# Channels outermost, heads innermost in the column blocks of a projection

## The chip, the cores and the metric

The kernel runs on one core of a Trainium2 chip. The metric is the device time of one execution in microseconds; of several runs the median counts.

## What is computed

One block of a diffusion backbone with 2048 latent tokens (`x`), a prefix of 256 context tokens (`ctx`) and 1024 channels: eight heads of a bidirectional RWKV-7 scan beside a gated short convolution, then a mixture of 16 experts that choose their tokens. The change touches only the first step, the projection, and what it leaves in DRAM for the scan. In short:

```python
px = modulate(rmsnorm(x, norm1_g), sh1, sc1) @ w_in        # the same for ctx
xr, xk, xv, xw, xa, xgl = split_rwkv(px_rw, mu, grid_shift(px_rw, rows))   # 512, 512, 512, 64, 64, 128 columns
kk = k * k_k;  kk = kk / max(sqrt(sum(kk * kk over a head)), 1e-12)
for d in (forward, backward):
    wl = -softplus(-(w0[d] + tanh(xw) @ w_up[d])) - 0.5
    a = sigmoid(a0[d] + xa @ a_up[d])
    kd = k * (1 + (a - 1) * k_a)
    y, s = wkv_scan(s0, r, exp(-exp(wl)), kd, v, -kk, kk * a, reverse=d)
bonus = sum(r * k_sum * r_k over a head) * v
...
x = x + g1 * (concat(a_x, b_x) @ w_out);  x = x + g2 * expert_choice_ffn(...);  return rmsnorm(x, final_g)
```

`grid_shift` moves channel 4i+t of a column to the left, right, upper or lower neighbour token, by its t.

## The kernel before

**Layout.** The projection keeps channels on the 128 partitions and tokens along the free dimension. On the host, `layout` reorders the columns of `w_in` into blocks of 128 (lines 1599 to 1608): block 0 holds the low-rank columns xw and xa, blocks 1 to 4 the keys, 5 to 8 the receptances, 9 the gate, 10 to 13 the values. The order inside a block is the list `tm` (line 1599): the shift t is outermost, so that a block has one shift direction, then the head h, then i, so that channel 4i+t of head h stands on partition 16h + i. The constants `mu`, `kk`, `ka`, `rk`, `w0`, `a0` follow the same list, and so do the columns of the low-rank matrices `wup2` and `aup2` (lines 1622 and 1623), whose rows are put in the order `perm64`.

**The passes.** `proj_phase` runs four passes of 512 tokens (the context's 256 go with the first). Each pass normalises and splits its tokens into a high and a low part (`prep_tile`), then runs 14 blocks: `load_block` (line 241) fetches the block's weights in two halves of 256 KB (tile `wr`, two buffers, line 247), ScalarE rounds them to `wH` (line 129), VectorE takes the rest as `wL` (line 134), and `block_mm` multiplies (line 262). What follows a block is queued and comes one block later: `post_wa`, `post_k`, `post_r` with `post_kd`, `post_g`, `post_v`. A timeline scheduler fixes the order of each engine's instructions when the program is built.

**The row stores.** `post_r` and `post_kd` leave in DRAM what the scan reads: `NR` (line 487; tiles `nrb` and `nrs`), and for both directions `C` (line 516; tile `ct`, two buffers) and `KBD` (line 517; tile `bk`, two buffers). A row there is one channel of one head over all 2304 tokens: 2304 floats in `C`, 2 x 2304 in `NR` and `KBD`. The destination's pattern is made by `to_heads` (line 373): the tile has 128 partitions, the DRAM side eight heads (64 rows apart) by 16 channels by the tokens. A buffer of `bk` is written first by VectorE at line 512, and may be written again once its store has landed; for `ct` that is the scan at line 508. All these DMAs are issued by the sync engine (SP), in program order, on one hardware queue that has the weight loads too, the stores `HS` of the normalised tokens (line 368), and the loads of `x`. In a pass the stores of blocks 5 to 8 follow one another, one block behind their blocks.

**The low-rank loads.** `post_wa` stores block 0 to `WA` (line 439) and reads it back twice onto two halves of 64 partitions (line 444), once for xw and once for xa; there the DRAM side has four shifts by 16 rows by the tokens.

**The values.** `post_v` turns values from channels on partitions to tokens on partitions (line 549), into a PSUM tile whose free order is shift, head, i. ScalarE copies it to the order head, shift, i (line 551), and it is stored to `V`.

Two small matrices pick heads: `bones` (128 x 128, ones where two partitions have the same head; line 322) and `hsel` (128 x 8; line 320), both from the partition number shifted right by four.

Of the kernel before, what the change touches and what calls it, by code (L numbers as in the profile page):

```python
# [7 lines left out]
F32 = mybir.dt.float32  # L8
# [5 lines left out]
OP = mybir.AluOpType  # L14
# [5 lines left out]
NTOK = T + TC  # L20
# [4 lines left out]
H = 8  # L25
# [17 lines left out]
def _dap(t, off, ap):  # L43
    a = t[tuple(slice(None) for _ in t.shape)] if not isinstance(t, bass.AP) else t
    return bass.AP(tensor=a.tensor, offset=a.offset + off, ap=ap)
# [220 lines left out]
def proj_phase(ctx_, tc, k, I, S, fill):  # L266
    nc = tc.nc
    bp = k.bp
    with ExitStack() as ctx:
# [42 lines left out]
        pi = pool.tile([128, 1], I32, name="pi", bufs=1)  # L312
# [1 line left out]
        bones = pool.tile([128, 128], F32, name="bones", bufs=1)  # L314
        hsel = pool.tile([128, H], F32, name="hsel", bufs=1)
        nc.gpsimd.iota(pi, pattern=[[1, 1]], base=0, channel_multiplier=1)
        nc.vector.tensor_scalar(pi, pi, 4, None, op0=OP.logical_shift_right)
        nc.vector.tensor_copy(pf, pi)
        nc.gpsimd.iota(jp, pattern=[[1, 128]], base=0, channel_multiplier=0)
        nc.vector.tensor_scalar(hsel, jp[:, 0:H], pf, None, op0=OP.is_equal)  # L320
        nc.vector.tensor_scalar(jp, jp, 4, None, op0=OP.logical_shift_right)
        nc.vector.tensor_scalar(bones, jp, pf, None, op0=OP.is_equal)
        up = pool.tile([128, 2, 2, 512], F32R, name="up", bufs=1)
        gupH = pool.tile([128, 512], F32R, name="gupH", bufs=1)
# [48 lines left out]
        def to_heads(t, j, mult, t0, n):  # L373

            w = mult * NTOK
            return _dap(t, j * 16 * w + mult * t0, [[64 * w, H], [w, 16], [1, mult * n]])

        def evac_lat(b, p, ps):
            e = pool.tile([128, 11, PR], F32, name="e")
# [51 lines left out]
        def post_wa(units, es):  # L431

            n0 = units[0][0]
            xx = [[pool.tile([128, 704], F32R, name="x" + nm + part, bufs=1) for part in "HL"] for nm in "wa"]
            for u, e in zip(units, es):
                t0, n, _ = u
                q = pool.tile([128, 512], F32, name="q")
                mixed(0, u, e, r64(q[:, :n]))
                nc.sync.dma_start(S["WA"][:, t0:t0 + n], q[:, :n])
                cs = slice(t0 - n0, t0 - n0 + n)  # L440
                for z in range(2):
                    q = pool.tile([128, 512], F32, name="q")
                    for half in range(2):
                        nc.sync.dma_start(q[64 * half:64 * half + 64, :n],
                                          _dap(S["WA"], 16 * z * NTOK + t0, [[32 * NTOK, 4], [NTOK, 16], [1, n]]))
                    if z == 0:
                        nc.scalar.activation(q[:, :n], q[:, :n], AF.Tanh)
                    split(k, nc, xx[z][0][:, cs], xx[z][1][:, cs], q[:, :n], "dve")
            xwa["x"], xwa["o"] = xx, n0
# [85 lines left out]
        def post_v(j, units, es):  # L535
            for u, e in zip(units, es):
                t0, n, _ = u
                big = n > 256
                if j == 0:
                    st["v", t0] = pool.tile([128, 4, 512 if big else 256], F32, name="kq" + "sb"[big], bufs=1)  # L540
                vq = st["v", t0]
                mixed(10 + j, u, e, r64(vq[:, j, :n]))
                if j < 3:
                    continue
                for a in range(0, n, 128):
                    m = min(128, n - a)
                    ps = psum.tile([128, 4, H, 16], F32, name="pw")
                    for i in range(4):
                        nc.tensor.transpose(ps[:m, i].rearrange("p h c -> p (h c)"), vq[:, i, a:a + m], k.ident)
                    v = pool.tile([128, H, 4, 16], F32, name="vt", tag="sg", bufs=2)  # L550
                    nc.scalar.copy(v[:m].rearrange("p h g c -> p g h c"), ps[:m])
                    vf = v.rearrange("p h g c -> p (h g c)")
                    nc.sync.dma_start(S["V"][t0 + a:t0 + a + m, :], vf[:m])
                    if t0 < TC:
                        continue
                    w = pool.tile([128, 512], F32, name="vb", tag="a", bufs=2)
                    nc.gpsimd.tensor_tensor(w[:m].rearrange("p (h c) -> p h c", c=C), v[:m].rearrange("p h g c -> p h (g c)"),
                                            st["o", t0][:m, a // 128].unsqueeze(2).to_broadcast([m, H, C]), op=OP.mult)
                    nc.vector.tensor_tensor(w[:m], w[:m], gn[:m, 1], op=OP.add)
                    nc.vector.tensor_tensor(w[:m], w[:m], st["g", t0][:m, a // 128], op=OP.mult)  # L560
                    nc.sync.dma_start(S["VB"][t0 - TC + a:t0 - TC + a + m, :], w[:m])
# [1019 lines left out]
def layout(inputs):  # L1581
    import numpy as np
    f = lambda n: np.asarray(inputs[n], dtype=inputs[n].dtype)
    g = {}
    perm64 = np.concatenate([np.arange(i, 64, 4) for i in range(4)])
    pm = lambda n: np.concatenate([perm64 + 64 * i for i in range(n // 64)])
    p512 = pm(512)
    g["x"] = np.ascontiguousarray(f("x").reshape(T, D))
    g["ctx"] = np.ascontiguousarray(f("ctx").reshape(TC, D))
    col = lambda v: np.asarray(v).reshape(-1, 128).T  # L1590
    ada_w, ada_b = f("ada_w")[0], f("ada_b")[0]
    g["ada_a"] = np.ascontiguousarray(ada_w[:, :2048].reshape(KT, 128, 2048))
    parts = [3, 4, 2, 5]
    g["ada_b"] = np.ascontiguousarray(
        np.stack([ada_w[:, o * 1024 + q * 512:o * 1024 + q * 512 + 512].reshape(KT, 128, 512) for o in parts
                  for q in range(2)]))
    g["ada_rows"] = np.ascontiguousarray(np.stack([ada_b[2048:3072], ada_b[5120:6144]]))
    w = f("w_in")[0]
    tm = np.array([h * 64 + 4 * i + t for t in range(4) for h in range(8) for i in range(16)])
    rw = np.concatenate([np.array([1536 + 64 * z + 4 * i + t for t in range(4) for z in range(2) for i in range(16)]),  # L1600
                         512 + tm, tm, np.array([1664 + 4 * i + t for t in range(4) for i in range(32)]), 1024 + tm])
    wr = w[:, :1792][:, rw]
    blocks = [wr[:, 128 * b:128 * b + 128] for b in range(14)]
    for j in range(4):
        for o in (2, 1, 0):
            s = 1792 + 512 * o + 128 * j
            blocks.append(w[:, s:s + 128])
    g["w_in"] = np.ascontiguousarray(np.stack([b.reshape(KT, 128, 128).transpose(1, 0, 2) for b in blocks]))
    mub = f("shift_mu")[0][rw]
    c = np.stack([f("c")[0].reshape(KT, 128), f("c_ctx").reshape(KT, 128)], axis=-1).transpose(1, 0, 2).reshape(128, 16)  # L1610
    cols = {"c": c, "adab_a": col(ada_b[:2048]), "adab_b": col(ada_b[3072:5120]), "n1": col(f("norm1_g")[0]),
            "n2": col(f("norm2_g")[0]), "mu": col(mub), "kk": col(f("k_k")[0][tm]), "ka": col(f("k_a")[0][tm]),
            "rk": col(f("r_k")[0].reshape(512)[tm]),
            "w0": np.concatenate([col(f("w0")[0, d][tm]) for d in range(2)], axis=1),
            "a0": np.concatenate([col(f("a0")[0, d][tm]) for d in range(2)], axis=1),
            "cw": np.concatenate([col(f("conv_w")[0, q]) for q in range(3)], axis=1)}
    colv = np.zeros((128, NCOLV), np.float32)
    for n, (a, b) in COLV.items():
        colv[:, a:b] = cols[n]
    g["colv"] = colv  # L1620
    dup = lambda u: np.ascontiguousarray(np.concatenate([u, u], axis=0))
    g["wup2"] = dup(f("w_lora_up")[0][:, perm64][:, :, tm].transpose(1, 0, 2))
    g["aup2"] = dup(f("a_lora_up")[0][:, perm64][:, :, tm].transpose(1, 0, 2))
    g["gup"] = np.ascontiguousarray(f("g_lora_up")[0][[4 * i + t for t in range(4) for i in range(32)]][:, p512])
    g["gnrows"] = np.ascontiguousarray(np.stack([f("gn_g")[0][p512], f("gn_b")[0][p512]]))
    g["router"] = np.ascontiguousarray(f("router_w")[0].reshape(KT, 128, NE).transpose(1, 0, 2))
    wo = f("w_out")[0]
    g["w_out"] = np.ascontiguousarray(np.concatenate([wo[:512][p512], wo[512:]]).reshape(KT, 128, D))
    for n, m in (("w_gate", "exp_w_gate"), ("w_up", "exp_w_up")):
        w = f(m)[0].reshape(NE, KT, 128, FB, 128).transpose(0, 3, 2, 1, 4)  # L1630
        g[n] = np.ascontiguousarray(w.reshape(NE, FB, 128, 1024))
    g["w_down"] = np.ascontiguousarray(f("exp_w_down")[0].reshape(NE, FB, 128, D))
    g["final_g"] = np.ascontiguousarray(f("final_g").reshape(1, D))
    return g
# [23 lines left out]
```

## Time and profile before

| | us |
|---|---|
| median of three runs | 3195.19 |
| lowest and highest of them | 3183.33, 3208.47 |
| the profiled execution | 3213.07 |
| its span from first to last instruction | 3211.1 |

The profiled execution is one execution of its own; the mean granted clock of TensorE in it is 0.921 of full speed. Its page lists for each engine the busy time, and the share of the 16 DMA engines' time in which they moved something. The projection takes the first 680 us of the span, the scan with its fillers goes to about 1930, the experts take the rest. PE is TensorE, DVE VectorE, ACT ScalarE, POOL GpSimd, SPq the sync engine's queue of issues.

### The profile page before, as it was taken

The numbers are of one execution on the slowest core, as the hardware profiler recorded it, in microseconds if no ns is written. First come the engines' busy times: TensorE is split into PE (matmuls) and PEld (weight loads), VectorE is DVE, ScalarE is ACT, GpSimd is POOL, SyncE is SP. The second block draws the span as 40 slices with busy tenths as digits, with TensorE's granted clock in tenths as the row PEclk, the third lists the DMA queues.
The fourth block names the chain that finished last, engine by engine and source line by source line (L and its number), as shares of the span: only waits on it lengthen the run. The fifth ranks groups of instructions, "written<-read, shape, count | busy, mean of one in ns | idle before, by whom it ended". The sixth has DMA issues, their size and how long they took to land. (4 is left out here: it accounts for less than half of the span.)

```text
span 3211.1 us, 62585 instructions
## 1 busy us (share of the span) xinstructions
PE 2904.7 (90%) x24367; PEld 2629.1 (82%) x24367; DVE 2136.1 (67%) x4611; ACT 1385.1 (43%) x2279; POOL 662.0 (21%) x893
## 2 busy tenths in 40 slices
PE   6878889878999998999999994999999999999997
PEld 4867778768888888877888873989999898999886
DVE  7567766758766666657767746666666666666766
ACT  6446554433344443323454433444444444444443
POOL 0132332443133323212222121001000000001001
PEclk8989899978799999998888986999999999999998
DMA  6355544575556665766566553566666666666786
GB/s 242 122 161 169 196 159 144 177 220 135 137 157 174 158 177 134 222 178 181 140 157 158 122 140 85 168 200 207 220 191 198 192 201 192 208 204 209 262 269 223
DMA packets 407497, 577.43 MB, mean 180 GB/s; under 512 B 174616, under 2 KB 256664, under 8 KB 406176
## 3 DMA queue, kind: packets, MB, share of 16 engines
q1 hardware_dynamic: 396256, 533.58, 54.9%
q0 software_dynamic: 10656, 38.80, 5.3%
q8 instruction: 191, 3.13, 0.4%
q14 instruction: 106, 0.87, 0.1%
q10 hardware_dynamic: 288, 1.05, 0.1%
HBM read 444.73 MB, written 128.59 MB: 179 GB/s over the span
## 5 line engine op out<-in xcount | busy, mean ns | idle before, releaser
L129 ACT CAST wH<-wr 128x1024 fp32r<-128x1024 f32 (+1 forms) x592 | 529.1, 897 | 907.3 <-PE pg L1429 409.4
L134 DVE TENSOR_TENSOR wL<-wr,wH 128x1024 fp32r<-128x1024 f32 (+1 forms) x586 | 625.7, 1072 | 363.4 <-ACT wH L129 358.4
L1429 PE MATMUL pg<-xH,wH 128*128 128x256 f32 x2048 | 587.8, 287 | 18.3 <-ACT s L1433 18.3
L1429 PE MATMUL pg<-xL,wH 128*128 128x256 f32 x2048 | 578.5, 283 | 0.0
L1429 PE MATMUL pg<-xH,wL 128*128 128x256 f32 x2048 | 578.1, 282 | 0.0
L262 PE MATMUL pj<-hH,wH 128*128 128x256 f32 x1600 | 482.1, 302 | 42.8 <-ACT wH L129 22.1
L262 PE MATMUL pj<-hH,wL 128*128 128x256 f32 x1600 | 472.5, 296 | 21.3 <-DVE wL L134 21.2
L262 PE MATMUL pj<-hL,wH 128*128 128x256 f32 x1600 | 471.6, 295 | 1.4 <-DVE hL L134 1.1
L1429 PEld LDWEIGHTS pg<-xH,wH 128*128 128x128 f32 x2048 | 392.1, 192 | 20.4 <-ACT s L1433 19.0
L1429 PEld LDWEIGHTS pg<-xL,wH 128*128 128x128 f32 x2048 | 391.5, 191 | 1.5
L1429 PEld LDWEIGHTS pg<-xH,wL 128*128 128x128 f32 x2048 | 391.9, 191 | 0.0
L262 PEld LDWEIGHTS pj<-hH,wH 128*128 128x128 f32 x1600 | 322.2, 201 | 56.7 <-ACT wH L129 26.3
L262 PEld LDWEIGHTS pj<-hH,wL 128*128 128x128 f32 x1600 | 320.0, 200 | 29.1 <-DVE wL L134 27.0
L262 PEld LDWEIGHTS pj<-hL,wH 128*128 128x128 f32 x1600 | 321.7, 201 | 5.7 <-DVE hL L134 2.0
L1488 POOL DMA_INDIRECT ACC<-o,it x30 | 52.0, 1732 | 968.9 <-DVE o L1474 809.4
L1446 PE MATMUL pd<-wH,hL 128*128 128x512 f32 x512 | 201.9, 394 | 0.0
L1446 PE MATMUL pd<-wL,hH 128*128 128x512 f32 x512 | 201.9, 394 | 0.0
L1446 PE MATMUL pd<-wH,hH 128*128 128x512 f32 x512 | 199.9, 394 | 0.0
L818 DVE TENSOR_TENSOR x<-X,x 128x120 f32<-128x120 f32 (+12 forms) x540 | 157.0, 294 | 58.3 <-DMA X<-TI 46.6
L820 DVE TENSOR_TENSOR X<-X,x 128x120 f32<-128x120 f32 (+12 forms) x540 | 164.8, 308 | 12.3
L782 PE MATMUL pg<-ar,bk 64*128 64x128 f32 x1152 | 136.3, 316 | 21.8 <-DVE g L784 8.1
L782 PEld LDWEIGHTS pg<-ar,bk 64*128 64x128 f32 x1152 | 110.1, 209 | 38.2 <-issue 13.9
(428 smaller groups left out, 5467.1 us busy)
## 6 DMA issues: line engine op xcount, KB each, us to landing
wr<-in_w_gate_dram SPq DMA_DIRECT2D x128, 512.0 KB
wr<-in_w_up_dram SPq DMA_DIRECT2D x128, 512.0 KB
wr<-in_w_down_dram SPq DMA_DIRECT2D x128, 512.0 KB
wr<-in_w_in_dram SPq DMA_DIRECT2D x208, 256.0 KB
bk<-KBD SPq DMA_DIRECT2D x36, 512.0 KB
ar<-NR SPq DMA_DIRECT2D x36, 512.0 KB
adaw<-in_ada_b_dram SPq DMA_DIRECT2D x32, 512.0 KB
inc<-C SPq DMA_DIRECT2D x36, 256.0 KB
```

The source lines that it names most:

```text
L129: nc.scalar.copy(H_, src)
L134: (leng or nc.vector).tensor_tensor(L_, src, H_.bitcast(F32), op=OP.subtract)
L262: nc.tensor.matmul(ps, wa[:, kw, :], ha[:, kt, :], start=m == 0, stop=m == 3 * KT - 1)
L782: nc.tensor.matmul(pg[:, p], bk[rows, p], ar[rows, p], start=True, stop=True)
L818: nc.vector.tensor_tensor(tv, X[:, 0:r, t:t + 1].to_broadcast([128, r, m]), x[:, t:t + 1, t + 1:].to_broadcast([128, r, m]), op=OP.mult)
L820: nc.vector.tensor_tensor(X[:, 0:r, t + 1:], X[:, 0:r, t + 1:], tv, op=OP.add)
L1429: nc.tensor.matmul(ps, a[:, ws], b[:, kt], start=i == 0, stop=i == 23)
L1446: nc.tensor.matmul(po[2 * m + n], a[:, f, ms], b[:, ns], start=f == 0 and q == 0, stop=f == FB - 1 and q == 2)
L1488: nc.gpsimd.indirect_dma_start(out=S["ACC"], out_offset=bass.IndirectOffsetOnAxis(ap=ids[m][:, :1], axis=0), in_=o, in_offset=None, comput ...
```

## The change

The list `tm` now has i outside and h inside: channel 4i+t of head h stands on partition 8i + h. All else follows from that. `to_heads` writes 16 channels by eight heads by the tokens; every row goes to the place in DRAM where it went before. The low-rank load reads 16 rows by four shifts by the tokens, so that the 64 partitions have the channels in their natural order, and `wup2` and `aup2` lose the row order `perm64`. The head of a partition is its number modulo 8 (`bitwise_and` with 7 in place of the shift). The PSUM tile of the transposed values has the free order shift, i, head, and the copy out of it reads in steps of eight elements.

```diff
--- before.py
+++ after.py
@@ -314,11 +314,11 @@
         bones = pool.tile([128, 128], F32, name="bones", bufs=1)
         hsel = pool.tile([128, H], F32, name="hsel", bufs=1)
         nc.gpsimd.iota(pi, pattern=[[1, 1]], base=0, channel_multiplier=1)
-        nc.vector.tensor_scalar(pi, pi, 4, None, op0=OP.logical_shift_right)
+        nc.vector.tensor_scalar(pi, pi, H - 1, None, op0=OP.bitwise_and)
         nc.vector.tensor_copy(pf, pi)
         nc.gpsimd.iota(jp, pattern=[[1, 128]], base=0, channel_multiplier=0)
         nc.vector.tensor_scalar(hsel, jp[:, 0:H], pf, None, op0=OP.is_equal)
-        nc.vector.tensor_scalar(jp, jp, 4, None, op0=OP.logical_shift_right)
+        nc.vector.tensor_scalar(jp, jp, H - 1, None, op0=OP.bitwise_and)
         nc.vector.tensor_scalar(bones, jp, pf, None, op0=OP.is_equal)
         up = pool.tile([128, 2, 2, 512], F32R, name="up", bufs=1)
         gupH = pool.tile([128, 512], F32R, name="gupH", bufs=1)
@@ -373,7 +373,7 @@
         def to_heads(t, j, mult, t0, n):
 
             w = mult * NTOK
-            return _dap(t, j * 16 * w + mult * t0, [[64 * w, H], [w, 16], [1, mult * n]])
+            return _dap(t, j * 16 * w + mult * t0, [[w, 16], [64 * w, H], [1, mult * n]])
 
         def evac_lat(b, p, ps):
             e = pool.tile([128, 11, PR], F32, name="e")
@@ -442,7 +442,7 @@
                     q = pool.tile([128, 512], F32, name="q")
                     for half in range(2):
                         nc.sync.dma_start(q[64 * half:64 * half + 64, :n],
-                                          _dap(S["WA"], 16 * z * NTOK + t0, [[32 * NTOK, 4], [NTOK, 16], [1, n]]))
+                                          _dap(S["WA"], 16 * z * NTOK + t0, [[NTOK, 16], [32 * NTOK, 4], [1, n]]))
                     if z == 0:
                         nc.scalar.activation(q[:, :n], q[:, :n], AF.Tanh)
                     split(k, nc, xx[z][0][:, cs], xx[z][1][:, cs], q[:, :n], "dve")
@@ -544,11 +544,11 @@
                     continue
                 for a in range(0, n, 128):
                     m = min(128, n - a)
-                    ps = psum.tile([128, 4, H, 16], F32, name="pw")
+                    ps = psum.tile([128, 4, 16, H], F32, name="pw")
                     for i in range(4):
-                        nc.tensor.transpose(ps[:m, i].rearrange("p h c -> p (h c)"), vq[:, i, a:a + m], k.ident)
+                        nc.tensor.transpose(ps[:m, i].rearrange("p c h -> p (c h)"), vq[:, i, a:a + m], k.ident)
                     v = pool.tile([128, H, 4, 16], F32, name="vt", tag="sg", bufs=2)
-                    nc.scalar.copy(v[:m].rearrange("p h g c -> p g h c"), ps[:m])
+                    nc.scalar.copy(v[:m].rearrange("p h g c -> p g h c"), ps[:m].rearrange("p g c h -> p g h c"))
                     vf = v.rearrange("p h g c -> p (h g c)")
                     nc.sync.dma_start(S["V"][t0 + a:t0 + a + m, :], vf[:m])
                     if t0 < TC:
@@ -1596,7 +1596,7 @@
                   for q in range(2)]))
     g["ada_rows"] = np.ascontiguousarray(np.stack([ada_b[2048:3072], ada_b[5120:6144]]))
     w = f("w_in")[0]
-    tm = np.array([h * 64 + 4 * i + t for t in range(4) for h in range(8) for i in range(16)])
+    tm = np.array([h * 64 + 4 * i + t for t in range(4) for i in range(16) for h in range(8)])
     rw = np.concatenate([np.array([1536 + 64 * z + 4 * i + t for t in range(4) for z in range(2) for i in range(16)]),
                          512 + tm, tm, np.array([1664 + 4 * i + t for t in range(4) for i in range(32)]), 1024 + tm])
     wr = w[:, :1792][:, rw]
@@ -1619,8 +1619,8 @@
         colv[:, a:b] = cols[n]
     g["colv"] = colv
     dup = lambda u: np.ascontiguousarray(np.concatenate([u, u], axis=0))
-    g["wup2"] = dup(f("w_lora_up")[0][:, perm64][:, :, tm].transpose(1, 0, 2))
-    g["aup2"] = dup(f("a_lora_up")[0][:, perm64][:, :, tm].transpose(1, 0, 2))
+    g["wup2"] = dup(f("w_lora_up")[0][:, :, tm].transpose(1, 0, 2))
+    g["aup2"] = dup(f("a_lora_up")[0][:, :, tm].transpose(1, 0, 2))
     g["gup"] = np.ascontiguousarray(f("g_lora_up")[0][[4 * i + t for t in range(4) for i in range(32)]][:, p512])
     g["gnrows"] = np.ascontiguousarray(np.stack([f("gn_g")[0][p512], f("gn_b")[0][p512]]))
     g["router"] = np.ascontiguousarray(f("router_w")[0].reshape(KT, 128, NE).transpose(1, 0, 2))
```

The instructions and their order stay as they were on PE, DVE, ACT and POOL, and on the sync engine too; what differs there is the pattern of the row stores. The first place is the start of the row stores in the first pass, in the sync engine's order; `nrs` and `nrb` are the context's and the latents' tiles of line 487, `ct` and `bk` those of lines 516 and 517, and the numbers are the outermost count, the next one and the elements of a row. Before:

```order
L444 DMA q<-WA 64x1x448 x4
L247 DMA wr<-in_w_in_dram 128x512 x8
L487 DMA NR<-nrs 8x16x512 x4
L247 DMA wr<-in_w_in_dram 128x512 x2
L516 DMA C_66<-ct 8x16x256
L517 DMA KBD_64<-bk 8x16x512
L247 DMA wr<-in_w_in_dram 128x512
L516 DMA C_67<-ct 8x16x256
L487 DMA NR<-nrb 8x16x896 x2
```

After, at the same place:

```order
L444 DMA q<-WA 64x1x448 x4
L247 DMA wr<-in_w_in_dram 128x512 x8
L487 DMA NR<-nrs 16x8x512 x4
L247 DMA wr<-in_w_in_dram 128x512 x2
L516 DMA C_66<-ct 16x8x256
L517 DMA KBD_64<-bk 16x8x512
L247 DMA wr<-in_w_in_dram 128x512
L516 DMA C_67<-ct 16x8x256
L487 DMA NR<-nrb 16x8x896 x2
```

No row moved: the stores have 16 by 8 rows in place of 8 by 16, and the weight loads stand between the same stores. The low-rank loads are listed by their partitions, so their rows read alike.

The second place is the third pass, 512 tokens, on the sync engine, where weight loads alternate with the stores of the first receptance block. Before:

```order
L516 DMA C_66<-ct 8x16x512
L247 DMA wr<-in_w_in_dram 128x512
L487 DMA NR<-nrb 8x16x1024
L247 DMA wr<-in_w_in_dram 128x512
L516 DMA C_67<-ct 8x16x512
L487 DMA NR<-nrb 8x16x1024
L517 DMA KBD_64<-bk 8x16x1024
```

After:

```order
L516 DMA C_66<-ct 16x8x512
L247 DMA wr<-in_w_in_dram 128x512
L487 DMA NR<-nrb 16x8x1024
L247 DMA wr<-in_w_in_dram 128x512
L516 DMA C_67<-ct 16x8x512
L487 DMA NR<-nrb 16x8x1024
L517 DMA KBD_64<-bk 16x8x1024
```

Again only the pattern of the stores differs; rows are as long as before, 1024 floats in `NR` and `KBD` and 512 in `C`.

## Rows read from the trace of the kernel before

**Rows 1.** The page's first line.

```profile
span 3211.1 us, 62585 instructions
```

**Rows 2.** Table of stretches: span, busy us per engine (instructions), TensorE's clock, DMA share, GB/s.

```profile
core 0: us, PE busy (x) PEld busy (x) DVE busy (x) ACT busy (x) POOL busy (x), PEclk, DMA share, GB/s
128.00:222.00 94.00, 70.97 (x486) 66.59 (x484) 65.17 (x88) 37.97 (x73) 33.59 (x38) 0.90 0.53 157
222.00:292.00 70.00, 62.87 (x411) 56.08 (x412) 44.40 (x75) 43.60 (x76) 13.28 (x31) 0.86 0.53 173
292.00:362.00 70.00, 52.53 (x290) 46.65 (x290) 54.10 (x68) 35.74 (x63) 30.57 (x29) 0.78 0.62 198
362.00:436.00 74.00, 69.46 (x530) 64.52 (x529) 46.32 (x77) 47.09 (x83) 15.72 (x33) 0.98 0.45 151
436.00:500.00 64.00, 51.09 (x322) 46.68 (x321) 53.33 (x59) 23.42 (x41) 34.35 (x31) 0.87 0.55 185
500.00:556.00 56.00, 51.99 (x412) 49.71 (x411) 36.56 (x66) 28.35 (x52) 10.59 (x31) 1.00 0.44 144
556.00:642.00 86.00, 73.04 (x520) 68.38 (x518) 65.77 (x110) 35.76 (x76) 34.55 (x46) 0.94 0.55 167
```

**Rows 3.** SP's issues by line: duration min/median/max in ns; weight loads from 100 us.

```profile
L247 SPq DMA_DIRECT2D wr<-in_w_in_dram x116: 327/333/2419, 100.2 to 673.8; - x116
L487 SPq DMA_DIRECT2D NR<-nrb x16: 565/612/2290, 137.6 to 581.6; - x16
L487 SPq DMA_DIRECT2D NR<-nrs x8: 565/623/1272, 121.5 to 582.6; - x8
L516 SPq DMA_DIRECT2D C<-ct x48: 565/585/3195, 131.2 to 633.3; - x48
L517 SPq DMA_DIRECT2D KBD<-bk x48: 565/579/2609, 135.2 to 637.7; - x48
L444 SPq DMA_DIRECT2D q<-WA x24: 507/528/690, 53.1 to 540.8; - x24
```

**Rows 4.** SP's timeline in the second store stretch: start us, duration us, issue.

```profile
328.73 2.22 SPq L247 DMA_DIRECT2D wr<-in_w_in_dram  x1
...
337.23 2.20 SPq L517 DMA_DIRECT2D KBD<-bk  x1
339.54 6.13 SPq L368 DMA_DIRECT2D HS<-htmp  x2
```

**Rows 5.** DMA issues of the projection by tile: count, KB each.

```profile
KBD<-bk SPq DMA_DIRECT2D x16, 512.0 KB
...
C<-ct SPq DMA_DIRECT2D x16, 256.0 KB
NR<-nrb SPq DMA_DIRECT2D x8, 512.0 KB
```

**Rows 6.** Waits from 40 to 680 us: who for whom, us in total, times, longest.

```profile
ACT wH L129 <- DMA wr<-in_w_in_dram: 130.4, 44, 7.4
DVE bk L512 <- DMA KBD<-bk: 43.2, 24, 4.8
...
PE pj L262 <- ACT wH L129: 22.1, 12, 3.4
PE pj L262 <- DVE wL L134: 21.2, 18, 3.0
ACT L447 <- DMA q<-WA: 13.3, 4, 5.4
...
DVE ct L508 <- DMA C<-ct: 5.9, 6, 3.5
DVE xaH L133 <- DMA q<-WA: 5.5, 4, 1.6
...
PE pw L503 <- DVE xwH L133: 2.4, 1, 2.4
```

**Rows 7.** The copy at line 551, by its line: duration min/median/max in ns.

```profile
L551 ACT COPY vt<-pw x19: 562/588/602, 228.2 to 664.0; 128x512 f32<-128x512 f32 x17, 64x512 f32<-64x512 f32 x2
```

## The prediction

> **What bounds the kernel now.** I read the table of stretches first, then the sync engine's DMA issues, then the waits. The whole program spans 3211.1 us [rows 1]; the change touches its first 680 us, the projection, and nothing behind it. There the table [rows 2] shows two kinds of stretch. Where a pass works on blocks 10 to 13 and 0 to 4, TensorE is busy for 62.87 of 70 us, 69.46 of 74 and 51.99 of 56, that is 0.90, 0.94 and 0.93, on average 0.92: those are TensorE's own. Where a pass works on blocks 5 to 8 and issues its row stores (128 to 222, 292 to 362, 436 to 500, 556 to 642 us, together 314 us) TensorE is busy 0.75, 0.75, 0.80 and 0.85 and VectorE 0.69, 0.77, 0.83 and 0.76. No engine is full there. The DMA share is 0.53 to 0.62, so half of the 16 DMA engines' time seems free.
>
> The sync engine shows that it isn't. A weight load (128 outermost rows) usually takes 0.33 us to issue, at worst 2.42 [rows 3]; the worst ones are in store stretches, where within 15 us a weight load takes 2.22, a KBD store 2.20 us, and two HS stores 6.13 us from the first's start to the second's end [rows 4]. An issue that takes nearly seven times its usual time is one that finds no room. The same view sorts issues by their DRAM pattern: 0.33 us with 128 outermost rows, 0.58 to 0.61 with eight (NR, C, KBD), 0.53 with four (the low-rank load). So transfers with few outermost rows are treated differently, and I read it as: eight outermost rows go to eight DMA engines.
>
> That can be tested on volume. In a 512-token pass each block stores 512 KB of NR, two KBDs of 512 and two Cs of 256 [rows 5], 2048 KB, so four blocks 8.39 MB; pass 0 has 704 tokens (11.53 MB), pass 3 576 (9.44 MB). The first store stretch moved 157 GB/s x 94 us = 14.76 MB at a share of 0.53, that is 8.48 engines at 18.5 GB/s each. With the stores on eight engines and the rest on 16, each of the eight carries 11.53/8 + 3.23/16 = 1.643 MB, 88.8 us of 94. The same sum gives 69.7 of 70, 60.1 of 64 and 78.4 of 86: 297.0 of 314 us. Eight engines would be 95% busy. That is too good for chance, and I take those eight engines as the bound of the store stretches.
>
> The waits say who pays. VectorE stands 43.2 us in front of line 512 until a KBD store has left its buffer and 5.9 us in front of the scan for a C store; ScalarE waits 130.4 us for weight rows, which land only when the busiest engine has delivered; TensorE waits 22.1 and 21.2 us for the two halves of the split weights [rows 6].
>
> **The change part by part.** Instructions and their order are the same on all five engines; what changes is inside the DMAs and one copy.
>
> *Stores, 120 of them (24 NR, 48 C, 48 KBD).* Same bytes, same row length, now 16 outermost rows. Spread evenly, the four stretches need 14.76 MB/16/18.5 GB/s = 49.9 us of DMA time, then 43.4, 35.2 and 47.3, together 175.8 of 314. DMA stops being the bound, and the next one is the busier of TensorE and VectorE. I let it reach the 0.92 that TensorE has between the stretches. Then the lengths are 70.97/0.92 = 77.1 (TensorE), 54.10/0.92 = 58.8 (VectorE), 53.33/0.92 = 58.0 (VectorE) and 73.04/0.92 = 79.4 us (TensorE): 273.3 instead of 314, so -40.7 us. This fits what it replaces, the 49.1 us of VectorE's waits for stores.
> The slow end: with two engines nearly level each waits for the other, and the best that any engine reaches in a store stretch now is TensorE's 0.85 in the last one. With 0.85 the lengths are 83.5, 63.6, 62.7 and 85.9, together 295.7: -18 us. The fast end: the granted clock in these stretches is 0.90, 0.78, 0.87 and 0.94; if idling brings it down and it rose to full, TensorE's busy time would fall to 63.9, 41.0, 44.4 and 68.7, VectorE would set the first three, and at 0.92 the sum is 262.3: -52 us. I take 0.92, since the stretches between are the same code on the same engines.
> The issue itself becomes cheaper if 16 outermost rows cost what 128 do: 120 x 0.25 = 30 us of sync engine. That queue sets nothing once it has room, so it is counted at nothing.
>
> A rule of the Trainium skill stands behind my reading: the page "DMA: Bandwidth & Descriptors", section "Why a DMA increments its semaphore by 16 and not by 1", says that a transfer uses the largest number of engines, at most 16, that divides the slowest dimension of both its patterns. By it the stores go from 8 to 16 engines and the sum is the one above. Without it the stores could stay where they are, which is a rival below; the volume test agrees with the rule, but no row here has an outermost 16.
>
> *Low-rank loads, 24 of them.* They go from four outermost rows to 16. ScalarE waits 13.3 us for them and VectorE 5.5, but TensorE only 2.4 us behind VectorE [rows 6]; most of this is latency that stays. Between 0 and -19 us; I take -2, the row nearest to TensorE.
>
> *The copy behind the V transposes, 19 of them.* ScalarE now reads PSUM in steps of eight elements. No row shows such a read; the same copy with plain reads takes 588 ns [rows 7]. It isn't cheaper for the same elements, so the ends are 0 and, if it doubles, 19 x 0.588 = +11 us. It runs where ScalarE is busy 43.60 of 70 us, so I take 0. If ScalarE's slack there were gone, the +11 would be paid.
>
> *The selectors and the low-rank weights' row order* change values only: 0.
>
> Sum: -40.7 - 2 = -42.7 us. The profiled execution took 3213.1 us, so 3170.4 for one like it. It lay 17.9 above the median of the three runs (3195.2); I forecast against the median: 3152.5, so 3153.
>
> **The rivals.**
> *The next bound is just behind.* TensorE and VectorE keep tripping over each other, and the stretches stay at 0.85: -18 us, 3177. For it: the last store stretch has TensorE at 0.85 although VectorE waits for stores there too. Against: between the stretches 0.92 is reached with the same splits.
> *The change doesn't do what it says.* If the outermost count doesn't decide the engines, stores stay as crowded: 3195. For it: no row of a 16-row pattern. Against: the issue times sort by just this count, and the volumes fill eight engines.
> *Slower: the rows collide in DRAM.* Today one engine writes the 16 neighbouring channels of a head, 18,432 B apart (2 x 2304 x 4); afterwards it writes one channel of eight heads, 64 x 18,432 = 1,179,648 B apart. If such rows took twice as long, the evenly spread 175.8 us would become 351.6, 37.6 more than now: 3233. It decides from a factor of 314/175.8 = 1.79. For it: no row has such steps within one engine. Against: today's eight engines together already write eight heads at that distance.
> [...]
>
> **How the numbers follow.** The forecast gets 0.61, with a range of its own of 3127 to 3170; the next bound 0.27; no effect 0.08; the collision 0.04. The median of three runs can be off by some 10 us, as they spread over 25. The range goes from the fast end with both small gains (3195 - 52 - 6 - 12 = 3125) to the slow end plus that spread (3177 + 12 = 3189); outside are the last two and a tail of the forecast, under 0.2. A measurement of this kernel can tell about 1% from no change, 32 us. Below 3163: most of the forecast's case and a little of the next, 0.58. Above 3227: the collision, 0.04. The rest is 0.38.
>
> **What would show it.** Right: issues of NR, C and KBD stores near 0.33 us instead of 0.58, low-rank loads likewise; VectorE's wait for KBD stores under 10 us; ScalarE's wait for weight rows cut by more than half; the store stretches some 273 us long with a DMA share near 0.64; the program behind the projection as long as before. Wrong: waits for stores gone but TensorE still under 0.85 there (then the wait has moved to VectorE or GpSimd); the share unchanged with stretched issues (the engines didn't change); or packets that take longer with a share near 1 (the collision).

## The result, and the profile after

| | before | after |
|---|---|---|
| median us (lowest to highest) | 3194.41 (3183.33 to 3208.47) | 3154.19 (3142.96 to 3155.36) |
| ratio, 95% interval | | 0.9864 (0.9819 to 0.9909) |
| span of the profiled execution | 3211.1 | 3141.1 |
| projection, to the scan's first load | 675.8 | 618.3 |
| behind the projection | 2535.3 | 2522.7 |

The median fell by 40 us, from four executions of each kernel, where 42.7 were forecast; on two other chips of this study it fell by 57 and 61 (e6 and e1). One execution of e3 and one of e5 took 5263 and 7352 us, which count in the medians below but not in the ratios. The profiled executions show the place: the projection. Its end is the first load of `C` for the scan, the first of the two last numbers in this row of the changed kernel's view by tile (675.8 in the kernel before):

```profile
L740 SPq DMA_DIRECT2D inc<-C x36: 359/380/1644, 618.3 to 1653.0; - x36
```

The table of stretches of the changed kernel, the four with row stores and one between; columns as in [rows 2]:

```profile
126.00:201.00 75.00, 64.54 (x478) 60.83 (x477) 65.75 (x89) 36.96 (x72) 38.24 (x38) 0.98 0.66 192
...
270.00:324.00 54.00, 43.44 (x277) 39.43 (x276) 53.11 (x65) 33.48 (x60) 33.35 (x29) 0.87 0.82 258
324.00:397.00 73.00, 69.60 (x537) 64.56 (x536) 48.59 (x80) 47.72 (x84) 16.39 (x34) 1.00 0.46 152
397.00:450.00 53.00, 41.52 (x271) 37.92 (x270) 50.22 (x54) 20.42 (x35) 34.84 (x30) 0.90 0.70 212
...
512.00:583.00 71.00, 65.43 (x489) 62.83 (x488) 65.61 (x104) 34.59 (x71) 34.30 (x43) 0.95 0.67 197
```

Read the third engine column (DVE) first. VectorE, which stood at 0.69 to 0.83 in the four stretches with row stores, is now at 0.88, 0.98, 0.95 and 0.92. In the two middle ones it is nearly full, as no engine was before; in the first and the last, TensorE is about as busy (0.86 and 0.92). The DMA share rose from 0.53 to 0.62 to between 0.66 and 0.82, since the same bytes pass in less time. And the granted clock rose from 0.78 to 0.87 in the second stretch and from 0.90 to 0.98 in the first.

The waits of the changed kernel, from 40 to 618 us, against [rows 6]:

```profile
ACT wH L129 <- DMA wr<-in_w_in_dram: 54.2, 26, 5.2
...
PE pj L262 <- DVE wL L134: 22.6, 18, 3.6
...
ACT L447 <- DMA q<-WA: 6.7, 3, 3.5
...
PE pj L262 <- ACT wH L129: 3.2, 5, 1.4
...
DVE bk L512 <- DMA KBD<-bk: 3.0, 4, 1.8
...
DVE xaH L133 <- DMA q<-WA: 0.7, 1, 0.7
```

VectorE's wait for KBD stores went from 43.2 us to 3.0, ScalarE's for weights from 130.4 to 54.2, TensorE's for the high halves from 22.1 to 3.2. TensorE's wait for the low halves stayed (21.2, now 22.6): those are VectorE's to make. The sync engine's issues by line, against [rows 3]:

```profile
L487 SPq DMA_DIRECT2D NR<-nrb x16: 517/554/2030, 135.8 to 533.6; - x16
...
L516 SPq DMA_DIRECT2D C<-ct x48: 517/524/1845, 128.2 to 576.8; - x48
...
L517 SPq DMA_DIRECT2D KBD<-bk x48: 517/524/1566, 133.9 to 580.4; - x48
...
L444 SPq DMA_DIRECT2D q<-WA x24: 520/586/637, 51.1 to 495.0; - x24
```

The longest issue of a row store is shorter (2.0 us, where it was 3.2; 2.6 in e1), but the usual one is 0.52 us and not the 0.33 of a load with 128 outermost rows.

### The profile page after: what moved, and what is told of

The parts are those of the page before. It is cut to its first block, busy times and chain, and to the rows that moved or that the text cites. A ratio compares the mean times of both kernels' runs of the same rounds, so it can differ in the third digit from the quotient of the medians.

```text
span 3141.1 us, 62585 instructions
## 1 busy us (share of the span) xinstructions
PE 2881.8 (92%) x24367; PEld 2612.9 (83%) x24367; DVE 2141.5 (68%) x4611; ACT 1385.0 (44%) x2279; POOL 667.4 (21%) x893
## 5 line engine op out<-in xcount | busy, mean ns | idle before, releaser
L262 PE MATMUL pj<-hH,wL 128*128 128x256 f32 x1600 | 469.4, 294 | 23.6 <-DVE wL L134 22.6
```

The costliest lines, as they stand in the source:

```text
L262: nc.tensor.matmul(ps, wa[:, kw, :], ha[:, kt, :], start=m == 0, stop=m == 3 * KT - 1)
```

## The experiments

In all of them "stretches" is the sum over the four passes from the first issue of a row store (line 516 or 487) to the first issue of the gate's store (line 586), read from the sync engine's timeline; "projection" runs to the scan's first load, and "behind it" from there to the end of the span. The prediction's 314 us are four windows with rounded edges; by this rule the same stretches of the kernel before are 307.3 us.

| kernel | median us | ratio to before (95%) | projection | stretches | behind it |
|---|---|---|---|---|---|
| before | 3194.41 | 1 | 675.8 | 307.3 | 2535.3 |
| after | 3154.19 | 0.9864 (0.9819 to 0.9909) | 618.3 | 261.0 | 2522.7 |
| e1 after, other chip | 3135.96 | 0.9824 (0.9793 to 0.9854) | 616.2 | 258.5 | 2516.0 |
| e2 eight channels outermost | 3188.95 | 0.9981 (0.9951 to 1.0011) | 673.0 | 311.9 | 2514.3 |
| e3 stores undone | 3188.64 | 0.9988 (0.9956 to 1.002) | 672.6 | 308.8 | 2513.7 |
| e4 four channels outermost | 3312.09 | 1.0356 (1.0314 to 1.0397) | 801.0 | 420.3 | 2511.3 |
| e5 low-rank loads alone | 3187.92 | 0.9965 (0.9937 to 0.9993) | 668.4 | 307.6 | 2522.1 |
| e6 after, third chip | 3141.46 | 0.9815 (0.9769 to 0.9862) | 617.9 | 258.9 | 2519.4 |
| e7 after, kd on ScalarE | 3111.76 | 0.972 (0.9684 to 0.9757) | 593.2 | 244.5 | 2519.6 |
| e8 before, kd on ScalarE | 3161.24 | 0.9888 (0.9852 to 0.9923) | 658.4 | 294.0 | 2511.1 |
| e9 as e7 | 3107.58 | 0.9726 (0.9683 to 0.977) | 596.8 | 244.5 | 2512.1 |
| e10 before again, one execution | 3184.64 | | 680.2 | 310.6 | 2502.6 |

The ratio compares each row with the kernel before on the same chip; the last three columns come from one profiled execution. The projection and the stretches repeat within some 5 us for the same kernel (675.8 and 680.2, 307.3 and 310.6 for the kernel before); the last column, the same code in all, spreads over 33 us.

**e1, e6: the changed kernel again.** No edit.

> The changed kernel once more, beside the others of this set, as their measure. Every theory: 3154 us, some 40 below the kernel before, the projection about 618 us long, VectorE waiting for KBD stores about 3 us in all.

> The changed kernel on this chip, as the measure of the next one: 3135 to 3155 us, projection 616 to 618 us.

The projection and the stretches came out as expected (616.2 and 617.9, 258.5 and 258.9). The time of e1, 3135.96, is 18 us below the 3154 expected; both ratios are 0.982.

**e2: eight channels outermost.** It asks whether the count of outermost rows matters or the place of the rows. Partitions keep channels outermost, but in pairs, and the rows of a head in DRAM are reordered to match, so that each store has 8 by 16 rows:

```diff
-            return _dap(t, j * 16 * w + mult * t0, [[w, 16], [64 * w, H], [1, mult * n]])
+            return _dap(t, j * 8 * w + mult * t0, [[w, 8], [32 * w, 16], [1, mult * n]])
-    tm = np.array([h * 64 + 4 * i + t for t in range(4) for i in range(16) for h in range(8)])
+    tm = np.array([h * 64 + 4 * (2 * a + b) + t for t in range(4) for a in range(8) for h in range(8) for b in range(2)])
```

(The values keep their own list, and the head of a partition is its number shifted right by one, modulo 8.)

> The changed kernel with eight outermost rows in the stores again, but channels still outermost: a partition is 16a + 2h + b for channel 2a + b, and the DRAM rows of a head are reordered to match, so that a store is 8 channels by 16 rows. Theory of the engines (eight outermost rows use eight DMA engines, and these bound the store stretches): back to 3190 to 3197 us, projection about 675, VectorE waiting for KBD stores about 43 us, sync engine's issues stretched to over 2 us. Theory of the placement (what helped is that one DMA no longer walks through neighbouring channels of one head): stays within 10 us of 3154.

The stretches are back at 311.9, the time at 0.998 of the kernel before. The waits from 40 to 673 us, of this kernel:

```profile
ACT wH L129 <- DMA wr<-in_w_in_dram: 136.0, 43, 8.4
DVE bk L512 <- DMA KBD<-bk: 45.6, 23, 4.8
```

And its issues of the KBD stores, from 100 us:

```profile
L517 SPq DMA_DIRECT2D KBD<-bk x48: 575/583/3064, 133.2 to 633.3; - x48
```

Both are the waits of [rows 6] again, and an issue of a KBD store again takes up to 3.06 us (2.61 before). The theory of the placement falls: with channels outermost and eight of them, nothing is gained.

**e3: the stores undone.** The list for keys and receptances, `to_heads` and the selectors are those of before; low-rank loads and values stay changed.

```diff
-            return _dap(t, j * 16 * w + mult * t0, [[w, 16], [64 * w, H], [1, mult * n]])
+            return _dap(t, j * 16 * w + mult * t0, [[64 * w, H], [w, 16], [1, mult * n]])
```

> The changed kernel with the stores as before (heads outermost, 8 by 16), and with the new low-rank loads and the new copy of the values kept. Theory of the engines: 3190 to 3195 us, the low-rank loads alone keep at most a few us. Theory that the low-rank loads or the values make the gain: stays near 3154.

The wait from 40 to 673 us, of this kernel:

```profile
DVE bk L512 <- DMA KBD<-bk: 42.1, 25, 4.4
```

The stretches take 308.8 us, the time is 3188.64, and VectorE's wait for KBD stores is back: the stores carry the gain.

**e4: four channels outermost.** As e2, with `[[w, 4], [16 * w, 32], [1, mult * n]]`.

> As the one with eight channels outermost, but with four (4 channels by 32 rows). Theory of the engines: the four stretches need 166.7 + 122.2 + 110.0 + 140.5 = 539 us of four engines' time by the volumes of the kernel before (where eight engines needed 297 and the stretches took 314), so about 570 us in place of 314, and 3400 to 3450 in all. Theory of the placement: within 15 us of the one with eight channels outermost, up or down. If the outermost count only changes how long an issue takes: within 15 us of 3154.

The direction is right and clear (1.0356), the size is not: 420.3 us in place of 570. The waits of this kernel, 40 to 801 us:

```profile
ACT wH L129 <- DMA wr<-in_w_in_dram: 252.8, 51, 13.6
...
DVE bk L512 <- DMA KBD<-bk: 116.1, 36, 8.1
...
PE pj L262 <- ACT wH L129: 82.4, 19, 13.6
```

And its first stretch by its DMAs, from 126 to 250 us (packets, then the queue's share of 16 engines):

```profile
DMA packets 7269, 14.47 MB, mean 117 GB/s; under 512 B 398, under 2 KB 2867, under 8 KB 7264
...
q1 hardware_dynamic: 7264, 14.40, 33.1%
```

The same row of the kernel before, from 128 to 222 us:

```profile
q1 hardware_dynamic: 7568, 14.72, 53.0%
```

And of the changed kernel, from 126 to 201 us:

```profile
q1 hardware_dynamic: 7556, 14.32, 65.6%
```

A share of 33.1% of 16 engines for 124 us makes 657 us of packet time for 14.40 MB, 45.6 us per MB. The same sum gives 54.2 us per MB in the first stretch of the kernel before and 55.0 in that of the changed kernel. So with four engines storing, a MB took 16% less packet time there. Over the four stretches, each taken by its own ratio (0.84, 0.88, 0.90 and 0.87), my 539 us, which had kept the packet times of before, should have been some 470. What remains to the measured 420 isn't explained.

The order of the three counts is what the engines' theory asks: 420, 312, 259 us for 4, 8 and 16 outermost rows. The traces also show the engines themselves. They keep the start and the time of every DMA packet, so one can count how many are in flight at once. Over the four stretches the count is most often exactly 4 in e4 (64% of the time), 8 in the kernel before and in e2 (41% and 43%), and 16 in the changed kernel (26%; 14 to 17 for 53%).

**e5: the low-rank loads alone**, on the kernel before.

```diff
-                                          _dap(S["WA"], 16 * z * NTOK + t0, [[32 * NTOK, 4], [NTOK, 16], [1, n]]))
+                                          _dap(S["WA"], 16 * z * NTOK + t0, [[NTOK, 16], [32 * NTOK, 4], [1, n]]))
...
-    g["wup2"] = dup(f("w_lora_up")[0][:, perm64][:, :, tm].transpose(1, 0, 2))
-    g["aup2"] = dup(f("a_lora_up")[0][:, perm64][:, :, tm].transpose(1, 0, 2))
+    g["wup2"] = dup(f("w_lora_up")[0][:, :, tm].transpose(1, 0, 2))
+    g["aup2"] = dup(f("a_lora_up")[0][:, :, tm].transpose(1, 0, 2))
```

> The kernel before with the low-rank loads alone changed: 16 rows by four shifts, and the low-rank matrices in natural row order. Stores as before. Theory of the engines: the stretches with row stores stay at some 307 us in all; the time between them falls by some 2 us in each pass, as the two runs with eight outermost store rows and these loads show; 3187 to 3194 us. If the loads did nothing: 3196.

The stretches stay (307.6), the projection is 7.4 us shorter, and the interval of the ratio just leaves out 1. In e2 and e3, which have these loads too beside stores with eight outermost rows, the projection is only 2.8 and 3.2 us shorter than 675.8; that is within the 5 us by which it repeats. ScalarE's and VectorE's waits for these loads:

```profile
ACT L447 <- DMA q<-WA: 6.8, 3, 3.1
...
DVE xaH L133 <- DMA q<-WA: 0.2, 1, 0.2
```

They were 13.3 and 5.5 us [rows 6].

**e7, e9: VectorE relieved.** One of VectorE's steps in each direction, 48 of them, goes to ScalarE:

```diff
-                    nc.vector.tensor_scalar(kd, r64(a[:, :n]), cvs(k, "ka", j), omka[:, j:j + 1], op0=OP.mult,
-                                            op1=OP.add)
+                    nc.scalar.activation(kd, r64(a[:, :n]), AF.Identity, scale=cvs(k, "ka", j), bias=omka[:, j:j + 1])
```

> The changed kernel with the first step of kd (times k_a plus a constant, 48 instructions of about half a microsecond on VectorE) moved to ScalarE. If VectorE is now what bounds the stretches with row stores (the profile of the changed kernel has it nearly full there): these shrink by half to all of the 24 us moved, 3115 to 3130 us where the changed kernel has 3140. If TensorE or the waits between engines bound them: within 5 us of the changed kernel. The scheduler orders the program anew for it, which alone can move the time by some microseconds either way.

> The changed kernel with the move once more, on the same chip, as the measure of the one beside it: 3105 to 3115 us.

The median is 3111.76 beside 3141.46 for the changed kernel on the same chip, a little below the 3115 to 3130 expected; e9 has 3107.58, as expected. This is the fastest version of this study, at 0.972 of the kernel before. The stretches fell by 14.4 us, the projection by 24.7, so some of it lies between the stretches, where the scheduler has reordered the program. The four stretches of e7:

```profile
126.00:193.00 67.00, 62.39 (x483) 59.83 (x482) 58.70 (x73) 47.26 (x92) 31.60 (x38) 1.00 0.74 220
261.00:312.00 51.00, 41.58 (x273) 38.43 (x273) 48.30 (x53) 32.41 (x56) 31.38 (x30) 0.90 0.76 232
382.00:434.00 52.00, 39.65 (x281) 36.51 (x280) 48.56 (x54) 33.56 (x58) 29.86 (x30) 0.93 0.72 223
496.00:563.00 67.00, 64.28 (x502) 63.10 (x501) 56.12 (x88) 45.03 (x88) 32.53 (x43) 0.97 0.70 213
```

VectorE is still the fullest engine in the second and third (0.95 and 0.93), with less to do. But these two, where it had been fullest, fell least: measured from issue to issue as in the table, the four stretches fell from e6 to e7 by 6.7, 2.8, 0.5 and 4.4 us (6.1, 2.7, -0.4 and 6.1 in e9). So the move shows that VectorE's work is on the path of the projection. That VectorE alone sets the two middle stretches is not shown.

**e8: the same move on the kernel before.**

> The kernel before with the same 48 instructions moved to ScalarE; its order of instructions is that of the changed kernel with this move, only the patterns of stores and low-rank loads are the old ones. If eight DMA engines bound the stretches with row stores in the kernel before, taking work from VectorE gains little there: 3185 to 3200 us, stretches about 300 us in all, and the change itself is then worth some 75 us. If VectorE bounded them already: 3165 to 3175 us, the same 25 to 30 us as on the changed kernel.

This missed: 3161.24 lies below what both theories gave. The time fell to 0.9888. By the medians the move brought 31 us here and 30 on the changed kernel. By the profiled executions the stretches fell by 13.3 us here and 14.4 there, the projection by 17.4 here (21.8 against e10) and 24.7 there. So the move is worth about as much with eight storing engines as with 16; that it is worth less here isn't shown. There is more waiting for KBD stores than before, now by two engines (40 to 658 us):

```profile
ACT bk L512 <- DMA KBD<-bk: 62.8, 26, 7.0
DVE bk L514 <- DMA KBD<-bk: 36.9, 20, 7.7
```

So the eight engines were no hard floor under the stretches as they stood. Counting packets in flight, and no more than eight at once, those eight were busy at most 0.92 of the stretches in the kernel before and 0.93 here, not the 0.95 of the prediction's volumes; how that little room gave 13 us isn't explained. With the move, the change is worth 62 to 65 us of projection (658.4 against 596.8 and 593.2) and 54 us by the medians on this chip; without it, 57.5 us of projection and 40 to 61 by the medians. The 75 us expected didn't come.

**e10: the kernel before again**, one profiled execution, no edit.

> The kernel before once more, with a profile. Its first profile had 2535 us behind the projection, where the runs since have 2511 to 2523 with the same code there. If that was one slow execution: projection again 670 to 680 us, 2510 to 2525 behind it, 3185 to 3200 in all, so that the change's gain lies in the projection alone. If the kernel before is truly slower behind the projection: 2530 or more there.

The projection repeats (680.2), and the part behind it takes 2502.6 us where the first profile had 2535.3. So the long part of the first profile belongs to that one execution, whose 3213.07 us are above the four of its set (3183.33 to 3208.47). No effect of the change behind the projection is seen beyond this spread. Another execution of the same kernel on this chip, without a profile, took 3205.07 us.

## Why the prediction was right, and where it was not

*Eight outermost rows use eight DMA engines, and these bound the stretches.* Right in the count, and nearly in the bound. The count is shown by e2 and e4: it alone, with the channels outermost in both, brings the stretches to 312 and 420 us, and the packets in flight are most often 8 and 4. As a bound it was softer than "95% busy" said: e8 shortened the stretches with eight engines too. By the Trainium skill's page "DMA: Bandwidth & Descriptors", section "Why a DMA increments its semaphore by 16 and not by 1", the number of engines follows from the slowest dimension; the three counts, 4, 8 and 16, agree with it.

*Stores: -40.7 us.* Right in mechanism, too small in size: the stretches fell by 46.3 in the first pair of profiles, and by 48 to 49 in e1 and e6. What was off is the 0.92 at TensorE's old busy time. VectorE reached 0.98 and 0.95 in the two middle stretches, and part of what the fast end had assumed came: the granted clock rose from 0.90, 0.78, 0.87 and 0.94 to 0.98, 0.87, 0.90 and 0.95, not to full. TensorE's busy time in the second stretch fell from 52.53 to 43.44 us, with 277 matmuls in the shorter window instead of 290. It isn't shown what raised the clock; the waits went and the clock rose in the same stretches. One sign that the prediction had named for being wrong did show: in the two middle stretches TensorE stays under 0.85 (0.80 and 0.78) with the waits for stores gone. But there the sum already had VectorE set the length.

*Low-rank loads: -2 us.* Small, and near what can be told: -7.4 in the projection by e5, -2.8 and -3.2 by e2 and e3. I had taken TensorE's own wait of 2.4 us, the row nearest to it; ScalarE and VectorE waited 19 us, and some of that may have come back. Of the first pair's 57.5 us, 11 lie outside the stretches; how many of them are these loads isn't shown.

*The copy of the values: 0.* Right, by the row that the prediction asked for: 562/586/602 ns for the 19 copies, 562/588/602 before [rows 7].

```profile
L551 ACT COPY vt<-pw x19: 562/586/602, 205.4 to 606.5; 128x512 f32<-128x512 f32 x17, 64x512 f32<-64x512 f32 x2
```

A step of eight elements in PSUM costs ScalarE nothing here.

*The issues at 0.33 us.* Wrong. With 16 outermost rows an issue takes 0.52 us, and that of the low-rank load became longer, 0.53 to 0.59. No cost of it is seen: VectorE's waits for KBD stores are 3.0 us all the same.

*The sum: -42.7.* The first comparison gave -40, the two others -57 and -61, and the projection is 57.5 shorter in the first pair of profiles. So the sum was some 15 us too small, 6 to 8 in the stores and the rest outside them. That the first median came within 2 us of the forecast is luck: the spread behind the projection, 33 us for one code, hides the difference in a single comparison. All three medians lie in the range.

*The rivals.* "No effect" and the placement fall by e2 to e4. The collision didn't come: with rows 1.18 MB apart a MB takes 55.0 us of packet time in the first stretch, against 54.2 before. In the Trainium skill's page "DMA: Bandwidth & Descriptors", section "Latency and other measured facts", the rates that fall are for row pitches at large powers of two, and 4 KiB of padding brings the full rate back at 4 MiB. 1,179,648 B is no power of two, and no run here shows such a fall. The next bound did come, with VectorE at 0.88 to 0.98, but later than that rival had it.

## What to carry to other kernels

A DMA share near one half with issues that take several times their usual time, and buffers that come free late, can be eight nearly full engines and eight mostly idle ones. Look at the outermost count of the transfers' patterns, and check it by volume: bytes per engine over the rate of a busy engine, against the length of the stretch. The count of packets in flight shows it directly where a trace has them. When such a limit goes, read the next one in the same table; here it was VectorE. Moving 48 small instructions off it brought another 30 us, and nearly the same, 31, before the change.

## What the runs showed that I had not expected

- An issue's time doesn't follow the outermost count: 0.33 us for weight loads of 128 plain rows, 0.52 for the C and KBD stores of 16 by 8 rows, 0.58 for those of 8 by 16, and for the low-rank loads, of 64 rows, 0.53 for 4 by 16 and 0.59 for 16 by 4.
- With fewer storing engines a MB takes less packet time: 45.6 us with four, 54.2 with eight, 55.0 with 16 in the first stretch. The usual packet is as long in all three, 84 ns at the median for 2048 bytes; what differs are the long ones: of the packets of 3584 bytes there, 3% take more than twice their median of 140 ns with four engines, 14% with eight, 22% with 16.
- Two limits can hold at once: relieving VectorE brought the kernel before as much by the medians (31 us) as the changed one (30), although its eight storing engines were up to 0.92 busy.
